# A two-layer hybrid decoder step: cached latents expanded by plain fp32 products, and four loops of small products in another order

## The chip, the core and the metric

The kernel runs on one core of a Trainium2 chip: TensorE (PE in the profile; PEld is its weight load), VectorE (DVE), ScalarE (ACT), GpSimd (POOL) and SyncE (SP), which here only issues transfers. The metric is the device time of one execution in microseconds, lower is better. The programs are compared by the median of several runs.

## What is computed

One inference step of two layers for 256 prompt tokens and 64 sample tokens (8 sequences of 8), model width 1024. Each layer projects its input for four mixers (latent attention, a convolution module, spatial gating and RWKV-7), projects their outputs back, and adds cross-attention to a memory and a gated feed-forward. Two pieces matter here. The sample tokens attend to 2048 cached positions each, which lie as latent rows of 512 columns in pages of 128 behind a page table; keys are expanded from the latents and normalised per head:

```python
def mla_expand(ckv, p):
    k_nope = rmsnorm((ckv @ p['mla_w_uk']).reshape(*lead, MLA_HEADS, QK_NOPE), p['mla_gk_nope'])
    v = (ckv @ p['mla_w_uv']).reshape(*lead, MLA_HEADS, V_DIM)

def mla_scores(q_nope, q_pe, k_nope, kpe):
    s = jnp.einsum('bqhd,bkhd->bhqk', q_nope, k_nope) + jnp.einsum('bqhr,bkr->bhqk', q_pe, kpe)
    return s.astype(jnp.float32) * MLA_SCALE

    def page_step(carry, phys):            # in mla_attend_sample, scanned over the page table
        m, l, acc = carry
        ckv_p = cache_ckv[phys, layer]
        kpe_p = cache_kpe[phys, layer]
        kn_p, v_p = mla_expand(ckv_p, p)
        sp = mla_scores(q_nope, q_pe, kn_p, kpe_p)
        m_new = jnp.maximum(m, jnp.max(sp, axis=-1, keepdims=True))
        corr = jnp.exp(m - m_new)
        ep = jnp.exp(sp - m_new)
        ...
```

And the sample tokens attend to 256 cached memory tokens with 4 heads of 128:

```python
    s = jnp.einsum('bthd,bmhd->bhtm', q, mem_k).astype(jnp.float32) * (X_HEAD_DIM ** -0.5)
    pr = jax.nn.softmax(s, axis=-1)
    xo = jnp.einsum('bhtm,bmhd->bthd', pr.astype(mem_v.dtype), mem_v)
```

All inputs and outputs are fp32.

## The kernel before

A layer goes through these stages: the combined projection and the mixers (rows by tag N, R, A, B, C), the scan of the paged cache with the rest of the mixers put between its steps (tags S and A), the output projection, cross-attention (tags X, Y and W; for the prompt's memory K and M) and the feed-forward (F). Dense products run in fp32r: a matrix is split into a high and a low part, and a product is the sum of three (high by high, low by high, high by low); `split` and `halves` make the parts with a ScalarE cast and a subtraction on VectorE or GpSimd. Products whose operands are plain fp32 tiles appear in the profile as two records each.

The scan (`mla_sample`, L1298) makes 8 steps in each layer, (g, Q) with g a half of the sequences and Q a quarter of their pages. `scan(g, Q)` takes 4 sequences j. For each it fetches the page rows (`Scb`, an indirect transfer issued by GpSimd, L1326) and the transposed latents (`Sckt`, 128x512, four transfers of 64 KB issued by SyncE, L1332, after the page numbers are read into registers). It casts the latents to fp32r (`Sckh`, ScalarE, L1336) and subtracts for the low part (`Sckl`, GpSimd, L397). For u in 0, 1 (two heads each) and j it expands them by three fp32r products into `pS`, and ScalarE squares the result into `Ssq`; the squares are summed per head by a product with 32 columns of weights into `pZ` (pZ<-Ssq), at partitions 32j to 32j + 31, so that the four j use four column groups of the array. The scores come from a second 32-column product, pZ<-Sckt. VectorE and ScalarE turn both into the scores `Sra`.

`attend` adds the rotary scores (16 products pA<-Scb,Akeep of 32 columns by 128), takes the running maximum and the exponentials, transposes them (pA<-fix,Sra), copies them to `Ak` (L1419) and multiplies them by the page rows (16 products pA<-Scb,Ak). `scan` of the next step is issued before `attend` of this one. The other mixers' VectorE work of that time is above all the causal convolution, one accumulation into `Bkeep` per tap (L401 for the prompt, L1000 for the samples).

In cross-attention the samples' queries are multiplied by cached memory keys (L1584: 16 products of 32 columns by 256 for each of two halves, pY and pZ<-u,Xm) and the weights by cached memory values (L1598: pY<-u,Ycc and pZ<-u,Wcc, 32 by 512). Both kinds of tile come through a ring of 13 buffers, `u`. The RWKV state loop (L877) makes 32 small products from the state of the sample sequences.

The order on each engine is set by a scheduler, from the program order and the waits that it models; `hold` keeps an instruction back in the schedule without a wait on the chip.

Of the kernel before, what the change touches and what calls it, by code (L numbers as in the profile page):

```python
# [10 lines left out]
F32 = mybir.dt.float32  # L11
# [12 lines left out]
NT = 320  # L24
# [297 lines left out]
def body(nc, tc, a, nl=L):  # L322
# [10 lines left out]
    BUFS = dict(u=13, wr=3, wh=4, wl=4, Nh=8, Nf=2, Nsm=2, Fh=8, Ff=4, Fsm=2, Xh=8, Xm=5, Xf=2, Xk2=2, Xcc=2, Xsm=8, Yk2=2, Ycc=2, Ysm=2,  # L333
# [24 lines left out]
    def block(tag, n):  # L358
        """one tile for what lives as long; returns what hands out its columns"""
# [20 lines left out]
    def in_order(first, last):  # L380
        """keeps the streamed products in program order among themselves"""
        after(first, dense_last[0])
        dense_last[0] = last
# [3 lines left out]
    def hold(ins, prev):  # L387
        """not before prev, by the schedule alone"""
        if prev is not None:
            tc.add_manual_dep(ins.ins, prev.ins.name, LATER, reason="held back")  # L390
# [43 lines left out]
    def keep(n):  # L434
        """columns held for the whole launch"""
# [29 lines left out]
    def rsq(e, now=False):  # L465
        """e <- e ** -0.5"""
# [12 lines left out]
    def split(hi, lo, src, scale=None, eng=None):  # L479
        """hi + lo = src * scale, both in fp32r"""  # L480
# [7 lines left out]
    def halves(raw, spans, scales=None, pool=()):  # L488
        """raw: a loaded tile, spans: column ranges -> (hi, lo) for each"""
# [15 lines left out]
    def wload(l, nm, idx, K):  # L505
        """one chunk of weights: a list of (hi, lo) [128, C] for its K row tiles"""
# [55 lines left out]
    def norm_pre(gain, wide=True):  # L562
        hs = []
        for k in range(8):
            h = sb("h", [128, 2, NT], F32R)
# [23 lines left out]
    def late():  # L589
        """what the first products do not need"""  # L590
# [7 lines left out]
    def group_norm_T(oj, vec, g, tag="F"):  # L598
        """oj: token rows [128, 256] x 3 -> split transposes of the normalised, scaled rows, [128, 2, NT] x 2"""
# [18 lines left out]
    def layernorm64(yj, eps):  # L618
        """per token and 64 columns, in place, without gain"""
# [48 lines left out]
    def rwkv(l, xs, vec):  # L668
# [45 lines left out]
        # normalised removal key  # L714
# [26 lines left out]
        # bonus  # L741
# [20 lines left out]
        # token rows of v, b and k  # L762
# [28 lines left out]
        # products between steps of a chunk  # L791
# [22 lines left out]
        # inverse of the unit triangular blocks by doubling  # L814
# [19 lines left out]
        for lev in (2, 4, 8, 16, 32):  # L834
# [4 lines left out]
            for q in qs:  # L839
# [5 lines left out]
                # the blocks of this level: rows of the first halves, columns of the second  # L845
# [19 lines left out]
        # state, chunk by chunk  # L865
# [7 lines left out]
        for c in (4, 0, 1, 2, 3):  # L873
            qs = None
            if c == 4:
                pq = [ps("T"), ps("T")]
                for hf in range(2):  # L877
                    R = Br[hf]
                    for i in range(2):
                        for b in range(8):  # L880
# [63 lines left out]
    def rwkv_out(l, vec, y, lng, lnb, vt, bon, tg, g2):  # L944
        # head norm, bonus, gate
# [13 lines left out]
    def sigmoid(t, scale=1.0, src=None):  # L959
        """t <- 1 / (1 + exp(scale * src))"""  # L960
# [141 lines left out]
    def mla(l, pj, vec):  # L1102
# [40 lines left out]
        # queries, keys and values  # L1143
# [67 lines left out]
        # sample queries against latents  # L1211
# [68 lines left out]
    class Side:  # L1280
        """work that is put between the steps of another"""
# [16 lines left out]
    def mla_sample(l, vec, t, side):  # L1298
        rq, qp, qz, ckT, kpT, ckn, ukv = (t[n] for n in ("rq", "qp", "qz", "ckT", "kpT", "ckn", "ukv"))
        oT = t["take"](4, 64)  # L1300
        u2 = sb("uk", [128, 2, 256], F32R)
        uh, ul = u2[:, 0], u2[:, 1]
        hold(S.copy(uh, ukv[:, 0:256]), pages[0])
        tt(ul, ukv[:, 0:256], uh.bitcast(F32), SUB)
# [4 lines left out]
        lows = []  # L1309

        def scan(g, Q):
            """page rows, and their scores without the rotary part"""
            ch[0] = "S"
            cbs, cks, ckhl = [], [], []
# [5 lines left out]
            for ld in loads:  # L1320
                hold(ld, lows[-BUFS["Sckt"]] if len(lows) >= BUFS["Sckt"] else cpage)
            for j in range(4):
# [12 lines left out]
                hi, lo = sb("ckh", [128, 512], F32R), sb("ckl", [128, 512], F32R)  # L1335
                S.copy(hi, ck)  # L1336
                lows.append(tt(lo, ck, hi.bitcast(F32), SUB, G if j in [0, 1, 2, 3] else V))
                ckhl.append((hi, lo))
            pn = ps("Z")
            for u in range(2):  # L1340
                sqs = []
                us = slice(128 * u, 128 * u + 128)
                for j in range(4):
                    p = ps("F")
                    hi, lo = ckhl[j]
                    mm(p, uh[:, us], hi, True, False)
                    mm(p, ul[:, us], hi, False, False)
                    mm(p, uh[:, us], lo, False, True)
# [53 lines left out]
        def attend(g, d, cbs, ra):  # L1402
            nb, ls, acc = d["nb"], d["ls"], d["acc"]
            p = ps("F")
            for j in range(4):
# [361 lines left out]
```

## Time and profile before

| | |
|---|---|
| runs, median of 3 | 1381.34 us (1374.33 to 1381.94) |
| span of the profiled execution | 1383.1 us |
| busy share PE, PEld, DVE, ACT, POOL | 96%, 81%, 70%, 47%, 16% |
| mean granted TensorE clock | 0.970 |
| mean traffic | 137 GB/s, 189.52 MB |

The profile shows one execution; its times are counted from the first instruction. "Busy" is the time in which at least one instruction of a kind ran; a matmul's end is modelled, so that records in steady flow overlap, and what one costs is read from start to start.

### The profile page before, as it was taken

What the parts mean: (1) busy time and instruction counts of PE and PEld (TensorE: products, weight loads), DVE (VectorE), ACT (ScalarE), POOL (GpSimd) and SP (SyncE); (2) the same over time, 40 slices, a digit from 0 to 9 for tenths busy, and PEclk for the clock granted to TensorE, in tenths of its full rate; (3) what the DMA queues carried; (4) which work ended last, traced back from release to release, by engine and by line L of the source; (5) the groups of instructions that cost most, each with busy time, mean ns of one, the idle gap of its engine ahead of it and who ended that gap; (6) DMA issues with size and microseconds to landing.
All of it is one profiled execution on the core that took longest, in us unless ns stands there. A gap on an engine that the chain in (4) does not pass through costs nothing.

```text
span 1383.1 us, 25248 instructions
## 1 busy us (share of the span) xinstructions
PE 1330.9 (96%) x9032; PEld 1113.5 (81%) x9032; DVE 962.2 (70%) x2414; ACT 651.6 (47%) x1425; POOL 217.5 (16%) x280
## 2 busy tenths in 40 slices
PE   5999999999999999999999899999999989999998
PEld 5859765566796799999998597755668959999998
DVE  6879468767786666566786894698777957655663
ACT  4443236667554544434444432375674635442441
POOL 1201313553000000000012113135540000000000
PEclk9999799999999999999999997999999999999999
DMA  7320313454475544444652204134563823444433
GB/s 233 125 77 15 118 44 89 140 159 145 146 253 191 177 157 145 154 153 151 201 171 94 81 11 123 42 88 133 162 215 143 296 93 137 147 144 153 153 115 107
DMA packets 105486, 189.52 MB, mean 137 GB/s; under 512 B 21393, under 2 KB 58642, under 8 KB 105362
## 3 DMA queue, kind: packets, MB, share of 16 engines
q1 hardware_dynamic: 91040, 157.84, 34.6%
q0 software_dynamic: 5120, 20.98, 5.0%
q10 hardware_dynamic: 9202, 9.11, 2.3%
q8 instruction: 71, 1.16, 0.3%
q14 instruction: 53, 0.43, 0.1%
HBM read 182.12 MB, written 5.75 MB: 136 GB/s over the span
## 4 chain that ended last, share of the span: by engine, by line
PE 52%; issue 9%; DVE 2%; POOL 1%; DMA 1%; ACT 0%; SPq 0%; POOLq 0%; ACTq 0%
PE pD L375 38%; PE pR L375 5%; PE pS L375 2%; PE pA L375 2%; PE pZ L375 2%; PE pA L460 1%; DMA Sckt<-in_ckvT 1%; PE pR L460 0%; DVE Bkeep L401 0%; DVE u L401 0%; PE pE L460 0%; POOL Sckl L397 0%; DVE Ccv L401 0%; DVE u L397 0%; DVE Sz L401 0%
## 5 line engine op out<-in xcount | busy, mean ns | idle before, releaser
L482 ACT CAST wh<-wr 128x512 fp32r<-128x512 f32 (+1 forms) x448 | 252.4, 601 | 133.0 <-PE pD L375 83.9
L375 PE MATMUL pD<-Fh,wh 128*128 128x320 f32 x1408 | 310.5, 309 | 0.0
L397 DVE TENSOR_TENSOR wl<-wr,wh 128x512 fp32r<-128x512 f32 (+1 forms) x448 | 291.7, 674 | 11.4 <-ACT wh L482 9.8
L375 PEld LDWEIGHTS pD<-Fh,wh 128*128 128x128 f32 x1408 | 235.7, 188 | 0.0
L375 PE MATMUL pD<-Fh,wl 128*128 128x320 f32 x704 | 217.5, 309 | 0.0
L375 PE MATMUL pD<-u,wh 128*128 128x320 f32 x704 | 154.9, 309 | 0.0
L375 PEld LDWEIGHTS pD<-Fh,wl 128*128 128x128 f32 x704 | 132.2, 188 | 0.0
L375 PEld LDWEIGHTS pD<-u,wh 128*128 128x128 f32 x704 | 117.8, 188 | 0.0
L397 DVE TENSOR_TENSOR Ff<-pD,fix 128x320 f32<-128x320 f32 x88 | 43.2, 491 | 103.3 <-PE pD L375 100.9
L375 PE MATMUL pD<-u,wl 128*128 128x320 f32 x352 | 108.8, 309 | 0.0
L375 PE MATMUL pD<-Nh,wh 128*128 128x320 f32 x384 | 94.6, 326 | 13.8 <-ACT wh L482 13.8
L413 ACT ACTIVATE u<-Ff 128x320 fp32r<-128x320 f32 x44 | 20.8, 472 | 176.1 <-DVE Ff L397 176.1
L397 POOL TENSOR_TENSOR Sckl<-Sckt,Sckh 128x512 fp32r<-128x512 f32 x64 | 85.8, 1351 | 108.7 <-ACT Sckh L1336 91.7
L375 PE MATMUL pS<-Sckh,Auk 128*128 128x512 f32 x256 | 92.0, 432 | 4.3 <-DVE Sra L401 1.8
L413 ACT ACTIVATE Ssq<-pS 128x512 f32<-128x512 f32 x128 | 73.5, 594 | 45.3 <-PE pS L375 38.6
L397 DVE TENSOR_TENSOR fix<-fix,pD 128x320 f32<-128x320 f32 x80 | 38.8, 485 | 73.0 <-PE pD L375 72.3
L375 PEld LDWEIGHTS pD<-Nh,wh 128*128 128x128 f32 x384 | 66.8, 194 | 19.6 <-ACT wh L482 13.8
L375 PEld LDWEIGHTS pS<-Sckh,Auk 128*128 128x128 f32 x256 | 47.3, 197 | 36.4 <-issue 22.1
L401 DVE SCALAR_TENSOR_TENSOR Bkeep<-Bkeep,fix 128x256 f32<-128x256 f32 x120 | 74.5, 624 | 0.6
L1326 POOL DMA_INDIRECT Scb<-in_ckv,fix x64 | 63.4, 991 | 63.4 <-PE pR L375 23.3
L375 PE MATMUL pZ<-Ssq,fix 128*32 128x512 f32 x256 | 71.9, 654 | 1.3 <-ACT Sra L414 0.9
L375 PEld LDWEIGHTS pD<-u,wl 128*128 128x128 f32 x352 | 66.1, 188 | 0.0
(478 smaller groups left out, 2580.7 us busy)
## 6 DMA issues: line engine op xcount, KB each, us to landing
wr<-in_w SPq DMA_DIRECT2D x200, 512.0 KB
Sckt<-in_ckvT SPq DMA_DIRECT2D x256, 64.0 KB
u<-in_memK SPq DMA_DIRECT2D x32, 256.0 KB
u<-in_memV SPq DMA_DIRECT2D x32, 256.0 KB
wr<-in_w SPq DMA_DIRECT2D x16, 384.0 KB
wr<-in_memT SPq DMA_DIRECT2D x12, 256.0 KB
wr<-in_w SPq DMA_DIRECT2D x8, 352.0 KB
Rmk<-in_cst ACTq DMA_DIRECT2D x2, 704.0 KB
```

The costliest lines, as they stand in the source:

```text
L375: return T.matmul(out, lhsT=lhsT, rhs=rhs, start=start, stop=stop)
L397: return (eng or V).tensor_tensor(out=out, in0=in0, in1=in1, op=op)
L401: return V.scalar_tensor_tensor(out=out, in0=in0, scalar=scalar, in1=in1, op0=op0, op1=op1)
L413: return S.activation(out, in_, func, bias=bias, scale=scale)
L460: T.transpose(out, in_, ident[:n, :n])
L482: S.copy(hi, src)
L1326: ld = nc.gpsimd.indirect_dma_start(out=cb.rearrange("p i c -> p (i c)"), out_offset=None, in_=a["ckv"], in_offset=off)
```

## The change

1. The latents are expanded by one plain fp32 product with the weights as they are (`ukv`), instead of three fp32r products. The casts `Sckh`, the subtractions `Sckl` and the split of the weights (`Auk`) are gone: 64 casts on ScalarE, 64 subtractions on GpSimd and, once in each layer, a cast and a subtraction for the weights.
2. The loops of the rotary scores, of the memory keys, of the memory values and of the RWKV state products have their inner and outer loops exchanged, so that products which follow each other write to different 32-column (or 64-column) parts of the array. For the keys, four tiles are now loaded ahead of the eight products that read them.
3. The register loads of page numbers are held behind the score of two steps back instead of the low part of twelve tiles back.
4. The eight tiles of a normalised input are one tile with eight parts.

```diff
+        hall = sb("h", [128, 8, 2, NT], F32R)
         for k in range(8):
-            h = sb("h", [128, 2, NT], F32R)
+            h = hall[:, k]
...
-                for hf in range(2):
-                    R = Br[hf]
-                    for i in range(2):
-                        for b in range(8):
+                for i in range(2):
+                    for b in range(8):
+                        for hf in range(2):
+                            R = Br[hf]
...
-        u2 = sb("uk", [128, 2, 256], F32R)
-        uh, ul = u2[:, 0], u2[:, 1]
-        hold(S.copy(uh, ukv[:, 0:256]), pages[0])
-        tt(ul, ukv[:, 0:256], uh.bitcast(F32), SUB)
...
             for ld in loads:
-                hold(ld, lows[-BUFS["Sckt"]] if len(lows) >= BUFS["Sckt"] else cpage)
+                hold(ld, scored[-2] if len(scored) - base >= 2 else cpage)
...
-                hi, lo = sb("ckh", [128, 512], F32R), sb("ckl", [128, 512], F32R)
-                S.copy(hi, ck)
-                lows.append(tt(lo, ck, hi.bitcast(F32), SUB, G if j in [0, 1, 2, 3] else V))
-                ckhl.append((hi, lo))
...
-                    hi, lo = ckhl[j]
-                    mm(p, uh[:, us], hi, True, False)
-                    mm(p, ul[:, us], hi, False, False)
-                    mm(p, uh[:, us], lo, False, True)
+                    mm(p, ukv[:, us], cks[j])
...
-            for j in range(4):
-                for n in range(4):
+
+            for n in range(4):
+                for j in range(4):
                     mm(p[32 * j : 32 * j + 32, n * 128 : n * 128 + 128], qz[:, 4 * g + j, n], cbs[j][:, 4])
...
-                for j in range(4):
-                    for h2 in range(2):
+
+                for h2 in range(2):
+                    kbs = []
+                    for j in range(4):
                         kb = sb("u", [128, 512])
                         hold(nc.sync.dma_start(kb, a["memK"][l, 4 * g + j, :, h2 * 512 : h2 * 512 + 512]), ahead)
-                        for hh in range(2):
-                            h = 2 * h2 + hh
-                            mm(p[32 * j : 32 * j + 32, 0:256], qpad[g][:, j, h], kb[:, hh * 256 : hh * 256 + 256], h == 0, h == 3)
+                        kbs.append(kb)
+                    for hh in range(2):
+                        h = 2 * h2 + hh
+                        for j in range(4):
+                            mm(p[32 * j : 32 * j + 32, 0:256], qpad[g][:, j, h], kbs[j][:, hh * 256 : hh * 256 + 256], h == 0, h == 3)
...
-                for j in range(4):
-                    for m in range(2):
+                for m in range(2):
+                    for j in range(4):
                         vb = sb("u", [128, 512])
```

What the scheduler makes of it is read from the order of instructions; three places follow. The first is TensorE in layer 0, from the expansion for the third scan step (pS) to the rotary scores of the first attend (pA<-Scb,Akeep; Scb_2035 to Scb_2068 are the rows of the four sequences, x4 is four products in a row). Before:

```order
L375 MATMUL pS<-Sckh_2504,Auk_1999 128x512 x2
L375 MATMUL pS<-Sckl_2505,Auk_1999 128x512
L375 MATMUL pS<-Sckh_2471,Auk_1999 128x512 x2
L460 MATMUL pA<-fix,As_2202 64x128
L375 MATMUL pS<-Sckl_2472,Auk_1999 128x512
L375 MATMUL pS<-Sckh_2482,Auk_1999 128x512 x2
L375 MATMUL pZ<-Ssq_2513,fix 32x512
L375 MATMUL pA<-Akeep_1313,As_2206 128x128
L375 MATMUL pA<-Scb_2035,Akeep_1313 32x128 x4
L375 MATMUL pA<-Scb_2046,Akeep_1313 32x128 x4
L375 MATMUL pA<-Scb_2057,Akeep_1313 32x128 x4
L375 MATMUL pA<-Scb_2068,Akeep_1313 32x128 x4
```

After:

```order
L375 MATMUL pS<-Sckt_2392,Akeep_1306 128x512
L375 MATMUL pZ<-Ssq_2421,fix 32x512
L375 MATMUL pS<-Sckt_2399,Akeep_1306 128x512
L460 MATMUL pA<-fix,As_2160 64x128
L375 MATMUL pZ<-Sckt_2392,Akeep_1306 32x512
L375 MATMUL pA<-Akeep_1306,As_2164 128x128
L375 MATMUL pA<-Scb_2025,Akeep_1306 32x128
L375 MATMUL pA<-Scb_2032,Akeep_1306 32x128
L375 MATMUL pA<-Scb_2039,Akeep_1306 32x128
L375 MATMUL pA<-Scb_2046,Akeep_1306 32x128
L375 MATMUL pA<-Scb_2025,Akeep_1306 32x128
L375 MATMUL pA<-Scb_2032,Akeep_1306 32x128
```

The rotary products now go round the four sequences; the expansion is one product, and single 32-column products (pZ) stand between the full ones. The second place is TensorE in layer 0 at the memory keys (u_5005 and so on are key tiles, Xm the padded queries). Before:

```order
L375 MATMUL pY<-u_5009,Xm_4652 32x256
L375 MATMUL pY<-u_5013,Xm_4652 32x256 x2
L375 MATMUL pY<-u_5017,Xm_4652 32x256 x2
L375 MATMUL pY<-u_5021,Xm_4652 32x256 x2
L375 MATMUL pY<-u_5025,Xm_4652 32x256 x2
```

After:

```order
L375 MATMUL pY<-u_4724,Xm_4379 32x256
L375 MATMUL pY<-u_4726,Xm_4379 32x256
L375 MATMUL pY<-u_4728,Xm_4379 32x256
L375 MATMUL pY<-u_4730,Xm_4379 32x256
L375 MATMUL pY<-u_4724,Xm_4379 32x256
L375 MATMUL pY<-u_4726,Xm_4379 32x256
L375 MATMUL pY<-u_4728,Xm_4379 32x256
L375 MATMUL pY<-u_4730,Xm_4379 32x256
```

Two neighbours used to read one tile and write one column group; now four neighbours read four tiles. The third place is GpSimd in layer 0 from the low parts for the fifth scan step on (Sckl) to the page rows of later steps (Scb). Before:

```order
L397 TENSOR_TENSOR Sckl_2937<-Sckt_2931,Sckh_2936 128x512
L1326 DMA Scb_2464<-in_ckv,fix 128x640
L1326 DMA Scb_2475<-in_ckv,fix 128x640
L1326 DMA Scb_2486<-in_ckv,fix 128x640
L1326 DMA Scb_2497<-in_ckv,fix 128x640
L397 TENSOR_TENSOR Csm_2850<-Csm_2850,fix 128x3
L397 TENSOR_TENSOR Sckl_2948<-Sckt_2942,Sckh_2947 128x512
```

After:

```order
L397 TENSOR_TENSOR Rsm_1910<-Rsm_1910,fix 128x12
L397 TENSOR_TENSOR Csm_2712<-Csm_2712,fix 128x3
L1323 DMA Scb_2390<-in_ckv,fix 128x640
L1323 DMA Scb_2397<-in_ckv,fix 128x640
L1323 DMA Scb_2404<-in_ckv,fix 128x640
```

Between the indirect transfers only small operations are left on GpSimd.

## Rows read from the trace of the kernel before

**Rows 1.** Section 1 of the page: busy us (share of the span) xinstructions.

```profile
PE 1330.9 (96%) x9032; PEld 1113.5 (81%) x9032; DVE 962.2 (70%) x2414; ACT 651.6 (47%) x1425; POOL 217.5 (16%) x280
```

**Rows 2.** By stage: stretch, length, busy us of PE, PEld, DVE, ACT, POOL, clock, DMA share, GB/s.

```profile
280.00:320.00 40.00, 36.54 (x287) 22.80 (x282) 24.61 (x50) 23.36 (x49) 22.58 (x21) 0.91 0.63 177
...
920.00:960.00 40.00, 36.76 (x282) 22.35 (x284) 36.43 (x75) 23.89 (x55) 22.38 (x18) 0.94 0.33 95
```

**Rows 3.** PE's waits, 183 to 352 us: us in total, times, longest.

```profile
PE pS L375 <- DVE Sra L401: 1.0, 1, 1.0
PE pA L460 <- ACT Sra L414: 0.9, 1, 0.9
...
PE pE L460 <- DVE Bg L397: 0.7, 1, 0.7
PE pS L375 <- ACT Sckh L1336: 0.6, 1, 0.6
```

**Rows 4.** PE's waits, 883 to 1058 us.

```profile
PE pA L375 <- DVE Ak L1419: 3.2, 1, 3.2
...
PE pS L375 <- DVE Sra L401: 0.8, 1, 0.8
```

**Rows 5.** Order of time, VectorE, then GpSimd: start us, us, instruction, xcount [idle before].

```profile
947.59 3.36 DVE L401 SCALAR_TENSOR_TENSOR Bkeep<-Bkeep,fix 128x256 f32<-128x256 f32 x1
...
948.13 2.53 POOL L397 TENSOR_TENSOR Sckl<-Sckt,Sckh 128x512 fp32r<-128x512 f32 x2
```

**Rows 6.** Tile Bkeep (ns min/median/max); then the page's group (busy us, mean ns).

```profile
L401 DVE SCALAR_TENSOR_TENSOR Bkeep<-Bkeep,fix x120: 443/475/3360, 175.7 to 985.1; 128x256 f32<-128x256 f32 x120
...
L401 DVE SCALAR_TENSOR_TENSOR Bkeep<-Bkeep,fix 128x256 f32<-128x256 f32 x120 | 74.5, 624 | 0.6
```

**Rows 7.** Order of time, PE, at an expansion: two triples of fp32r products begin.

```profile
282.50 0.62 PE L375 MATMUL pS<-Sckh,Auk 128*128 128x512 f32 x2
...
283.19 0.62 PE L375 MATMUL pS<-Sckh,Auk 128*128 128x512 f32 x2
```

**Rows 8.** Order of time, PE, at a plain fp32 product of that shape.

```profile
83.34 1.02 PE L375 MATMUL pA<-Akeep 128*128 128x512 f32 x2
...
84.43 0.40 PE L375 MATMUL pD<-wl,Nh 128*64 128x512 f32 x1
```

**Rows 9.** Order of time, PE, at memory values and at products with page rows.

```profile
1040.38 1.08 PE L375 MATMUL pA<-Scb,Ak 128*32 128x128 f32 x32
1041.39 0.73 PE L375 MATMUL pK<-wh,Mh 128*128 128x512 f32 x2
...
1119.29 1.94 PE L375 MATMUL pY<-u,Ycc 128*32 128x512 f32 x16
1121.06 1.06 PE L375 MATMUL pZ<-u,Xm 128*32 128x256 f32 x8
```

**Rows 10.** Page, groups of instructions: busy us, mean ns, idle before and its releaser.

```profile
L397 POOL TENSOR_TENSOR Sckl<-Sckt,Sckh 128x512 fp32r<-128x512 f32 x64 | 85.8, 1351 | 108.7 <-ACT Sckh L1336 91.7
...
L413 ACT ACTIVATE Ssq<-pS 128x512 f32<-128x512 f32 x128 | 73.5, 594 | 45.3 <-PE pS L375 38.6
```

**Rows 11.** Groups of PE's instructions by line and shape, columns as in rows 10.

```profile
L375 PE MATMUL pA<-Scb,Akeep 128*32 128x128 f32 x512 | 42.8, 278 | 0.2
L375 PE MATMUL pA<-Scb,Ak 128*32 128x128 f32 x512 | 20.3, 297 | 4.0 <-DVE Ak L1419 4.0
L375 PE MATMUL pY<-u,Xm 128*32 128x256 f32 x64 | 12.4, 384 | 0.0
L375 PE MATMUL pZ<-u,Xm 128*32 128x256 f32 x64 | 12.1, 382 | 0.1
...
L375 PE MATMUL pY<-u,Ycc 128*32 128x512 f32 x32 | 3.9, 598 | 0.0
```

**Rows 12.** By stage in layer 1's cross-attention, columns as in rows 2.

```profile
1100.00:1110.00 10.00, 10.00 (x71) 6.47 (x70) 6.17 (x29) 2.93 (x10) 0.00 (x0) 1.00 1.00 364
...
1120.00:1131.00 11.00, 8.44 (x59) 3.81 (x51) 3.62 (x13) 4.03 (x11) 0.00 (x0) 1.00 0.00 0
```

More of the change, by code (lines that the diff above doesn't have):

```diff
@@ L332, in body @@
     RINGS = ("u", "Scb", "Sckt", "Sckh", "Sckl", "Ssq", "Sra", "Sz", "Ff", "Fh", "Nf", "Mf")
-    BUFS = dict(u=13, wr=3, wh=4, wl=4, Nh=8, Nf=2, Nsm=2, Fh=8, Ff=4, Fsm=2, Xh=8, Xm=5, Xf=2, Xk2=2, Xcc=2, Xsm=8, Yk2=2, Ycc=2, Ysm=2,
+    BUFS = dict(u=13, wr=3, wh=4, wl=4, Nh=1, Nf=2, Nsm=2, Fh=1, Ff=4, Fsm=2, Xh=1, Xm=5, Xf=2, Xk2=2, Xcc=2, Xsm=8, Yk2=2, Ycc=2, Ysm=2,
                 Rkeep=1, Rh=6, Rf=3, Rg1=3, Rk2=3, Rcc=3, Rs2=2, Rst=2, Rsh=1, Rsm=4,
@@ L1300, in mla_sample @@
         oT = t["take"](4, 64)
-        u2 = sb("uk", [128, 2, 256], F32R)
-        uh, ul = u2[:, 0], u2[:, 1]
-        hold(S.copy(uh, ukv[:, 0:256]), pages[0])
-        tt(ul, ukv[:, 0:256], uh.bitcast(F32), SUB)
         qf = lambda b: qp[:, b].rearrange("p h t -> p (h t)")
         PG = [0, 0, 3, 3]
-        lows = []
+        base = len(scored)
         def scan(g, Q):
             ch[0] = "S"
-            cbs, cks, ckhl = [], [], []
+            cbs, cks = [], []
             cpage = pages[[0, 2, 3, 3][min(2 * Q + g, 3)]]
```

## The prediction

> **What bounds the kernel now.** I read the page first. TensorE (PE) is busy for 96% of 1383.1 us and VectorE, ScalarE and GpSimd for 70, 47 and 16% [rows 1], so a change counts by what it takes from PE or adds to it, and by the waits of PE that it moves. Next I read the table by stage, for the stretches in which the kernel goes through the paged cache ("the scan" below; 183 to 352 us and 883 to 1058 us are the windows read). There PE is not full: 36.54 us of 280 to 320 and 36.76 of 920 to 960, and the granted clock is 0.91 and 0.94 there [rows 2]. A clock c over T us costs about T x (1 - c), since for part of T it is granted the lower level, 1.2 of 2.4 GHz, and work goes at half speed: 3.6 and 2.4 us for the two rows. Third, the waits of PE in the scan, by what ended them [rows 3, 4]: three rows of layer 0 name VectorE (1.0 to 0.7, together 2.5 us) and five of layer 1 (3.2 to 0.8, together 6.8 us), so 9.3 us in all. Rows that name ScalarE, six and four, come to another 6.3 us, from 0.9 down; one of 0.6 names the cast that the change removes.
>
> Why is VectorE late, when it is no more than 70% busy? The order of time shows it: an accumulation into Bkeep that has a median of 475 ns takes 3.36 us at 947.59, while GpSimd makes two of the Sckl tiles from 948.13 on [rows 5]. The longest of the 120 is this 3360 ns, and their mean is 624 ns, so this line alone is 120 x 0.149 = 17.9 us above its median [rows 6]. Adding up, over the trace, what VectorE's instructions take above the median of their own kind, I find 40 us in 44 instructions, and all 44 lie over an Sckl subtraction. The Ak copy that PE waits for (3.2 us) stands in VectorE's queue behind such a stretch.
>
> **The change part by part.** *Expansion of the latents.* Three fp32r products give way to one plain fp32 product, 128 times. In steady flow a triple starts every 283.19 - 282.50 = 0.69 us [rows 7], 0.23 us a product. A plain fp32 product of the same shape (128x512, weights 128x128, two records) stands elsewhere in the kernel: from its start at 83.34 to 84.43 lie it and one fp32r product, 1.09 us, so it takes 1.09 - 0.23 = 0.86 us [rows 8]. That is 0.17 us dearer: 128 x 0.17 = **+21.8 us**. Bounds: the pair is listed with 1.02 us from its first start to its last end, so if nothing overlapped its end the term would be 128 x 0.33 = +42; below 0.86 it can't go as long as PE has other work to take, since that row is steady flow already, and where PE stands still beside it the waits below take the difference up. I take 21.8.
>
> *Norm and score products (pZ, 32 columns of the array).* Their count is the same, but they are placed otherwise. Four that follow each other use four column groups and run as one pass: eight in pY<-u,Ycc take 1121.06 - 1119.29 = 1.77 us, 0.89 a pass [rows 9]. I counted passes over both program orders, a pass being a run without another kind of product between and without a column group twice: 35 before and 45 after in layer 0, 35 and 49 in layer 1. 24 x 0.89 = **+21.4 us**; the bound below is half, where PE would have sat waiting for the squares anyway. The array changes between 32-column and full products 71 times in each layer before, 79 and 91 after. One change back costs about 0.12 us: the 32 small records from 1040.38 fill 1.01 us [rows 9], and eight steps of a quarter of 0.44 us (half of 0.89) make 0.89. So 28 x 0.12 = **+3.4 us**. The Trainium skill, TensorEngine Tiling (Array Packing), section Key Properties, says that a change of tiling mode drains the engine; this speaks against the new order, and the trace agrees in sign, with 0.12 us a change. Also, six more norm products stand right behind the product that feeds their square. A square takes 594 ns [rows 10], so 0 to 3.6 us; I take **+2 us**.
>
> *Casts and subtractions.* 64 Sckh casts on ScalarE and 64 Sckl subtractions on GpSimd (85.8 us) go [rows 10]. They overlap PE, so their own time counts nothing; what comes back is what waited behind them. Of VectorE's 9.3 us I give back **-8 us** (one wait of 0.8 is for the RWKV mixer); of ScalarE's 6.3, whose queue gets shorter, **-3 us**; and the clock of the stretches 280 to 320 and 920 to 960, which falls right behind such waits, 3.6 + 2.4 = **-6 us** [rows 2]. Bounds: nothing of it, or all, 9.3 + 6.3 + 6.0 = 21.6 us. What is late next is then the chain of softmax, ScalarE's exponentials before the transposes, not the subtraction.
>
> *Rotary scores (pA<-Scb,Akeep).* 16 loops, whose order now cycles through the four column groups. The products with the values (pA<-Scb,Ak) have the same shape and count and already cycle: 20.3 us busy against 42.8 [rows 11]. **-22.5 us**; in the new order 15 of the 16 loops stand unbroken, so little of it is in doubt.
>
> *Cached memory keys (pY and pZ<-u,Xm).* 128 records of 256 columns, 12.4 + 12.1 = 24.5 us [rows 11]. The memory values run four at once: 32 records of 512 columns in 3.9 us, so 64 of 256 also 3.9, and 128 of them 7.8. Gain at most 16.7; the new order breaks some blocks, so that I count 24 passes for the 16 that are needed, eight more of 0.44 us, which leaves 13.2. In layer 1 the transfers are full until 1110 (share 1.00), and there PE may get ahead of its tiles; none is left after 1120 [rows 12]. I take off 1 more: **-12 us**, bounds -6 (half) and -13.2.
>
> *No term.* The values' loop already runs four at once (above), and in the RWKV state loop the program order is what it was: the scheduler had and has one half behind the other. The page-number loads now come after the score two scans back; that leaves one scan, some 20 us (a window of 170 holds eight), for its 16 loads of 64 KB, 1 MB, which the transfers move in about 3 us at 364 GB/s [rows 12].
>
> Sum: 21.8 + 21.4 + 3.4 + 2 - 8 - 3 - 6 - 22.5 - 12 = -2.9 us. The profiled span of 1383.1 is 1.8 above the runs' median of 1381.34; the difference is taken off the median: **1378 us** after rounding.
>
> **The rivals.** A measurement here can tell about 1% (13.8 us) from no change. (a) *Faster*: the new passes fall into time in which PE waited for squares anyway (10.7 instead of 21.4) and all the waits and clock come back: 21.8 + 10.7 + 3.4 - 21.6 - 22.5 - 13.2 = -21, **1360 us**. For it: all 44 long VectorE instructions have one cause, and it goes. The Trainium skill, SBUF — State Buffer, section SBUF: two separate sides, calls the port pair of VectorE and GpSimd an exclusive lock held for the whole instruction, for VectorE instructions with two SBUF inputs; the trace agrees, 3.36 us against 0.475. Against it: the waits named for VectorE are 9.3 us, not 40. (b) *Slower*: in the scan the norm pass is the new wait. Each single norm product takes a pass for itself and waits for its square, and PE is the limit there, so that no wait comes back: 21.8 + 21.4 + 3.4 + 3.6 - 22.5 - 6 = +22, **1403 us**. For it: +50 us of dearer work is certain, and its relief rests on waits; against it: the waits shown are caused by what is removed. It decides once less than 8 of the 17 us of waits and clock come back while the memory keys give 6. (c) *The turned loops don't do what they say*: the keys wait for transfers and the rotary loops gain half: the sum is then -2.9 + 11 + 6 = +14, 1395, the edge of "slower".
>
> **How the numbers follow.** The forecast, within 1% (1367 to 1395), 0.50; (a) and what lies toward it 0.31; (b) and (c) 0.19. The likeliest case alone is 1368 to 1391. The range goes a little past (a), which holds its clearest part, and to the edge of (c): 1356 to 1396; what lies beyond it is most of (b) and a tail of (a), some 0.18.
>
> **What would show it.** Right: pS<- Sckt at 0.86 us a product; the Bkeep line with a maximum near its median; pA<-Scb,Akeep near 20 us and pY and pZ<-u,Xm near 11 together; the clock 1.00 in the stretches that follow the waits. Wrong: pS records with gaps, waits of PE for Ssq by the dozen, PE waiting for loads of Sckt or of memory keys, or a Bkeep line still at 600 ns.

## The result, and the profile after

| | before | after |
|---|---|---|
| median of 20 runs each | 1379.89 us | 1387.07 us (1381.79 to 1396.14) |
| ratio to before, 95% interval | 1 | 1.0062 (1.0043 to 1.0081) |
| span of the profiled execution | 1383.1 us | 1384.6 us |
| mean granted clock | 0.970 | 0.979 |

The changed kernel is 0.6% slower, 8.6 us by the ratio: within 1% and inside the range, but on the other side of no change from the -2.9 us of the sum. Here is TensorE's work after, first section 1 of the page (as [rows 1]), then three stretches (columns as in [rows 2]):

```profile
PE 1337.6 (97%) x8904; PEld 1061.7 (77%) x8904; DVE 921.6 (67%) x2412; ACT 627.2 (45%) x1359; POOL 131.1 (9%) x216
```

```profile
280.00:320.00 40.00, 39.56 (x261) 16.24 (x261) 12.82 (x29) 20.78 (x40) 11.12 (x12) 1.00 0.59 175
...
920.00:960.00 40.00, 37.25 (x273) 15.77 (x271) 31.57 (x85) 18.75 (x39) 6.79 (x7) 1.00 0.51 154
...
1110.00:1120.00 10.00, 8.94 (x42) 3.62 (x44) 2.94 (x14) 1.34 (x5) 0.00 (x0) 0.66 0.56 191
```

In the two stretches of the scan the clock is 1.00 (it was 0.91 and 0.94) and PE is fuller by 3.0 and 0.5 us. The third, at the memory keys of layer 1, has a new dip to 0.66. VectorE's accumulation into Bkeep, the tile and its group (as [rows 6]):

```profile
L401 DVE SCALAR_TENSOR_TENSOR Bkeep<-Bkeep,fix x120: 448/478/485, 179.4 to 963.8; 128x256 f32<-128x256 f32 x120
```

```profile
L401 DVE SCALAR_TENSOR_TENSOR Bkeep<-Bkeep,fix 128x256 f32<-128x256 f32 x120 | 56.7, 476 | 0.0
```

The longest of the 120 is 485 ns instead of 3360. PE's waits, 183 to 365 us and then 880 to 1058 us (as [rows 3, 4]):

```profile
PE pZ L375 <- DVE Asm L401: 1.0, 1, 1.0
...
PE pZ L375 <- ACT Ssq L413: 1.0, 1, 1.0
...
PE pA L375 <- DVE Akeep L397: 0.8, 1, 0.8
PE pZ L375 <- DVE Bkeep L401: 0.7, 1, 0.7
```

```profile
PE pZ L375 <- ACT Ssq L413: 2.3, 2, 1.5
PE pA L375 <- DVE Akeep L1424: 1.1, 1, 1.1
```

VectorE is named with 3.6 us (2.5 and 1.1) instead of 9.3, and the Ak copy is no longer among them. So most of what was to be relieved was relieved, and the kernel is slower. Groups of PE's instructions (as [rows 10, 11]):

```profile
L375 PE MATMUL pS<-Sckt,Akeep 128*128 128x512 f32 x256 | 130.9, 621 | 1.8 <-DMA Sckt<-in_ckvT 0.9 <-PE pZ L375 0.8
L375 PE MATMUL pZ<-Ssq,fix 128*32 128x512 f32 x256 | 80.6, 603 | 5.0 <-ACT Ssq L413 3.2 <-DVE Asm L401 1.0 <-DVE Bkeep L401 0.7
L375 PE MATMUL pA<-Scb,Akeep 128*32 128x128 f32 x512 | 27.2, 276 | 0.0
L375 PE MATMUL pA<-Scb,Ak 128*32 128x128 f32 x512 | 18.0, 276 | 0.1
L375 PE MATMUL pZ<-u,Xm 128*32 128x256 f32 x64 | 9.0, 437 | 0.6 <-issue 0.6
L375 PE MATMUL pY<-u,Xm 128*32 128x256 f32 x64 | 5.5, 386 | 0.0
```

The rotary scores went from 42.8 to 27.2, not to 20.3, the keys from 24.5 to 14.5. Since busy times of neighbours overlap, I use from here on "own time": for each record of PE the time from its start to the start of the next one, added up by kind, over the scans of both layers. It also holds the time in which PE stood still behind a record, and what a lower clock added.

| own time, us | pS | pZ<-Ssq | pZ<-Sckt | rotary |
|---|---|---|---|---|
| before | 115.5 | 60.6 | 22.5 | 41.4 |
| after | 128.4 | 62.3 | 27.1 | 25.4 |
| e3 (one-tile norm input) | 110.2 | 59.8 | 19.4 | 42.6 |
| e1 (e3 and turned loops) | 109.5 | 65.4 | 19.8 | 24.8 |
| e2 (e3 and plain fp32) | 125.9 | 62.3 | 26.3 | 39.8 |
| e9 (e3, grouped) | 112.8 | 55.3 | 20.0 | 41.6 |
| e11 (e2, grouped) | 122.4 | 36.8 | 21.2 | 39.1 |
| e7 (after, grouped) | 124.3 | 37.4 | 20.3 | 24.3 |

### The profile page after: what moved, and what is told of

The parts are those of the page before. It is cut to its first block, busy times and chain, and to the rows that moved or that the text cites. A ratio compares the mean times of both kernels' runs of the same rounds, so it can differ in the third digit from the quotient of the medians.

```text
span 1384.6 us, 24573 instructions
## 1 busy us (share of the span) xinstructions
PE 1337.6 (97%) x8904; PEld 1061.7 (77%) x8904; DVE 921.6 (67%) x2412; ACT 627.2 (45%) x1359; POOL 131.1 (9%) x216
## 4 chain that ended last, share of the span: by engine, by line
PE 82%; issue 8%; DVE 3%; DMA 3%; ACT 1%; POOL 1%; SPq 1%; POOLq 0%; DVEq 0%; ACTq 0%
PE pD L375 48%; PE pR L375 10%; PE pS L375 7%; PE pZ L375 6%; PE pA L375 4%; PE pK L375 2%; PE pA L460 1%; DMA u<-in_memV 1%; DMA wr<-in_memT 1%; PE pR L460 1%; PE pX L375 1%; DVE u L401 1%; PE pE L460 1%; PE pE L375 1%; DMA Bkeep<-in_convh 0%
## 5 line engine op out<-in xcount | busy, mean ns | idle before, releaser
L482 ACT CAST wh<-wr 128x512 fp32r<-128x512 f32 (+1 forms) x448 | 257.6, 603 | 272.4 <-PE pD L375 188.9
L375 PE MATMUL pS<-Sckt,Akeep 128*128 128x512 f32 x256 | 130.9, 621 | 1.8 <-DMA Sckt<-in_ckvT 0.9
L375 PE MATMUL pZ<-Ssq,fix 128*32 128x512 f32 x256 | 80.6, 603 | 5.0 <-ACT Ssq L413 3.2
L375 PEld LDWEIGHTS pS<-Sckt,Akeep 128*128 128x128 f32 x256 | 42.8, 192 | 55.2 <-issue 37.6
L375 PE MATMUL pD<-Nh,wl 128*128 128x320 f32 x192 | 62.9, 327 | 2.2 <-DVE wl L397 2.2
L375 PE MATMUL pD<-wh,Nh 128*128 128x352 f32 (+3 forms) x192 | 59.2, 382 | 0.2 <-ACT u L413 0.2
```

The lines of the kernel that those rows point to most:

```text
L375: return T.matmul(out, lhsT=lhsT, rhs=rhs, start=start, stop=stop)
L482: S.copy(hi, src)
```

## The experiments

Each was timed in five rounds beside the kernel before on its own chip, and ratios are to that; 0.1% is 1.4 us, and "x% below e3" is a difference of two such ratios. Letters in the quoted expectations stand for theories; what each comes to is said in words behind it. The kernels come in four sets of four that shared a chip: e1 to e4, e5 to e8, e9 to e12, e13 to e16. The kernel before took 1379.8, 1384.0, 1388.2 and 1384.7 us on the four chips.

### The parts alone (e1 to e4)

e3 is the kernel before with the one-tile input of the norm and nothing else (its ring holds one such tile instead of eight small ones, as many columns):

```diff
+        hall = sb("h", [128, 8, 2, NT], F32R)
-            h = sb("h", [128, 2, NT], F32R)
+            h = hall[:, k]
```

> Only the one-tile norm input is changed, everything else as before. Theory A and B: nothing, ratio 1.000 within 0.002. Rival C (the single tile adds waits at the start of each normalised projection; in the changed kernel's trace layer 0 is 3.3 us later at its first expansion): +3 to +5 us, ratio 1.002 to 1.004.

Measured 0.996 (0.9938 to 0.9981). The part that should cost nothing gave 0.4%, 5.5 us, and not the loss of rival C; e1, e2 and e4 have it too, so they are compared with e3. By the traces PE's records stand in another order in places, most of them in the last part of each scan. The clock goes with it: its mean over all runs is 0.9763 in e3 and 0.9736 in the kernel before beside it, which by T x (1 - c) is 32.6 and 36.4 us, 3.8 of the 5.5. Why the order and the clock changed I did not settle.

e1 adds the four turned loops, of which this is the rotary one:

```diff
-            for j in range(4):
-                for n in range(4):
+            for n in range(4):
+                for j in range(4):
                     mm(p[32 * j : 32 * j + 32, n * 128 : n * 128 + 128], qz[:, 4 * g + j, n], cbs[j][:, 4])
```

> The four turned loops and the one-tile norm input, with the three fp32r products, casts and subtractions of before. Theory A (the loops gain what PE saves in them, and the plain expansion then costs more than its relief returns): by the trace of the changed kernel the rotary loops take 25.4 us instead of 41.4 and the keys 16.3 instead of 24.7, so about 24 us under before, ratio 0.982. Theory B (the expansion is about even and it is the loops that lose their gain, in waits for softmax and for key tiles): within 5 us of before, ratio 0.997 to 1.003.

Measured 0.9837 (0.9806 to 0.9869), as theory A said against the kernel before; against e3 it is 1.2% less, 17 us.

e4 is e3 with this loop alone turned.

> Only the rotary loop turned (and the one-tile norm input), fp32r expansion as before. Theory A: -16 us, as the 16 loops take 25.4 us instead of 41.4, ratio 0.988. Theory B: -5 to 0 us, because PE then waits for the exponentials that it used to cover.

Measured 0.9877 (0.9849 to 0.9905), again theory A's ratio; 0.8% below e3, 11.5 us, where its own time fell by 17.3. On the same chip e1 lies 0.4% under e4, 5.5 us (the intervals overlap), which is what the other three loops gave together.

e2 is e3 with the plain fp32 expansion, all loops as before. The later load of page numbers comes with it, since the low parts that the old hold names are gone; PE waits for latents (Sckt) for 0.9 us in all in the changed kernel, by the group of pS above.

```diff
-                    mm(p, uh[:, us], hi, True, False)
-                    mm(p, ul[:, us], hi, False, False)
-                    mm(p, uh[:, us], lo, False, True)
+                    mm(p, ukv[:, us], cks[j])
```

> The plain fp32 expansion without any turned loop (with the one-tile norm input and the later load of page numbers). Theory A: it carries the loss and the loops hide it, +7 + 24 = about 31 us over before, ratio 1.022; VectorE's long instructions are gone all the same. Theory B: about +5 us, ratio 1.004.

Measured 1.0165 (1.0136 to 1.0193), 2.05% above e3: 28 us, between the two theories and nearer A. With the loops turned (the changed kernel against e1) it is 2.25%, 31 us. The parts add up: -5.5 (e3), -17 (e1 against e3), +31 (after against e1) make the +8.5 of the whole.

### What the casts and subtractions were worth (e5, e8)

e5 is e2 with the 64 casts and 64 GpSimd subtractions made all the same, their results unused:

```diff
+                hi, lo = sb("ckh", [128, 512], F32R), sb("ckl", [128, 512], F32R)
+                S.copy(hi, ck)
+                tt(lo, ck, hi.bitcast(F32), SUB, G)
```

> The plain fp32 expansion without turned loops, and beside it the 64 casts and 64 GpSimd subtractions of before, whose results nothing reads. Theory A (the dearer products cost about 41 us in all, and 14 come back because the casts and subtractions are gone): the 14 are lost again, 1402 + 14 = 1416 us, ratio 1.026. Rival D (what comes back is small, the dearer products cost about 27 in all): 1402 to 1405 us, ratio 1.016 to 1.018.

Measured 1.0194 (1.0153 to 1.0235), 0.3% above e2, some 4 us with intervals that overlap: nearer rival D than A. VectorE's long instructions are back in it: what its instructions take above the median of their kind is some 26 us in over 30 instructions (40 us in the kernel before, none in the changed kernel). Since nothing reads the results, e5 prices the load on the two engines and their collision, not the chain from the latents over cast and subtraction to the product.

e8 is e1 with the subtractions on VectorE instead of GpSimd, so that the two engines can't meet there:

```diff
-                lows.append(tt(lo, ck, hi.bitcast(F32), SUB, G if j in [0, 1, 2, 3] else V))
+                lows.append(tt(lo, ck, hi.bitcast(F32), SUB, V))
```

> Four turned loops with the fp32r expansion, the low parts made by VectorE instead of GpSimd. Theory A: VectorE's 36 us of overlong instructions go, but 64 subtractions of about 0.68 us, 43 us, come: as the loops alone, 1358 us within 4, ratio 0.984. Rival H (what hurts is the single long stall in front of a wait of TensorE, and short ones more in number do not): 1345 us, ratio 0.975.

Measured 0.9815 (0.9774 to 0.9856), theory A's 0.984 and not to be told from e1's 0.9837. The tile Bkeep in e1 and then in e8 (min/median/max):

```profile
L401 DVE SCALAR_TENSOR_TENSOR Bkeep<-Bkeep,fix x120: 449/475/2054, 175.5 to 962.2; 128x256 f32<-128x256 f32 x120
```

```profile
L401 DVE SCALAR_TENSOR_TENSOR Bkeep<-Bkeep,fix x120: 463/476/483, 180.1 to 991.4; 128x256 f32<-128x256 f32 x120
```

The stalls vanish (2054 to 483 ns) and the time doesn't move. But VectorE takes on the 64 subtractions, and PE now waits for it in another place, 191 to 351 us in e8:

```profile
PE pZ L375 <- DVE Sra L401: 4.1, 2, 3.6
```

So e8 is a net, behind which a gain can hide. That the stalls cost a few us at most rests on e5; e8 does not contradict it.

### How the small products stand in the order (e7, e9 to e11)

The schedule of e7 keeps the four norm products of each u behind the last square of that u, and the score products behind the norm products; nothing else differs from the changed kernel:

```diff
-                    act(sq, p, AF.Square)
+                    held = act(sq, p, AF.Square)
...
-                    mm(pn[32 * j : 32 * j + 32], C("hsum")[:, 32 * u : 32 * u + 32], sqs[j], u == 0, u == 1)
+                    last = mm(pn[32 * j : 32 * j + 32], C("hsum")[:, 32 * u : 32 * u + 32], sqs[j], u == 0, u == 1)
+                    hold(last, held)
...
-                mm(p[32 * j : 32 * j + 32], qf(4 * g + j), cks[j])
+                hold(mm(p[32 * j : 32 * j + 32], qf(4 * g + j), cks[j]), last)
```

> The changed kernel, with the norm products held by the schedule until all four squares are made, and the score products behind the norms: 30 and 29 passes of 32-column products instead of 44 and 48, and 112 changes of array mode instead of 170. Theory A (each pass takes 0.89 us of TensorE, but grouping makes it wait for squares part of that time): about half of 33 x 0.89, -15, so 1372 us, ratio 0.994. Rival G (single passes lie in time in which TensorE waits anyway): no change, 1387 us, ratio 1.005. If every pass counts fully: 1355 us, ratio 0.982.

Measured 0.9789 (0.9749 to 0.9829): 2.7% below the changed kernel, 38 us. That is more than any theory gave; the interval takes in the 0.982 of every pass counted fully, and neither A nor G. By the table of own times pZ<-Ssq loses 24.9 us, pZ<-Sckt 6.8 and pS 4.1, together 35.8: nearly all of it. In the same stretch of time, order of time on PE, first the changed kernel, then e7:

```profile
283.98 2.84 PE L375 MATMUL pS<-Sckt,Akeep 128*128 128x512 f32 x6
286.76 1.37 PE L375 MATMUL pZ<-Ssq,fix 128*32 128x512 f32 x7
287.64 0.39 PE L375 MATMUL pA<-Scb,Akeep 128*32 128x128 f32 x6
287.97 0.59 PE L375 MATMUL pZ<-Ssq,fix 128*32 128x512 f32 x1
288.40 0.59 PE L375 MATMUL pZ<-Sckt,Akeep 128*32 128x512 f32 x1
```

```profile
286.69 1.03 PE L375 MATMUL pZ<-Ssq,fix 128*32 128x512 f32 x6
287.65 2.84 PE L375 MATMUL pS<-Sckt,Akeep 128*128 128x512 f32 x6
```

Six records of pS (three products) take 286.76 - 283.98 = 2.78 us. Behind them the changed kernel's small products come in runs of seven, six and one record, and a lone record takes 0.43 us (288.40 - 287.97); in e7 six of them take 0.96 together.

e11 is e2, e9 is e3 and e10 is e1 with the same lines.

> Plain fp32 expansion, loops not turned, grouped: 30 and 29 passes instead of 44 and 48, 112 changes instead of 170. Theory P: 33 x 0.89 + 58 x 0.12 = -36 against the plain expansion alone, ratio 0.990; the difference to the grouped fp32r kernel is then what the expansion itself costs without its fragments, about 0 to +18 us. Rival Q: as P here, but with the grouped fp32r kernel 30 us lower than this one.

> fp32r expansion, loops not turned, one-tile norm input, with the norm and score products grouped by the schedule: 31 and 32 passes of 32-column products instead of 34 and 37, and 114 changes of array mode instead of 144. Theory P (a pass costs 0.89 us and a change of mode 0.12 wherever they stand): 8 x 0.89 + 30 x 0.12 = -11 against the one-tile kernel, ratio 0.988. Rival Q (grouping is worth as much as in the changed kernel, for another reason, such as the wait for a single square): -30, ratio 0.975.

> The same grouping with the four loops turned, fp32r expansion: 30 and 32 passes instead of 34 and 37, 118 changes instead of 140. Theory P: 9 x 0.89 + 22 x 0.12 = -11 against the loops alone, 1347 us, ratio 0.976. Rival Q: -30, 1328 us, ratio 0.962.

| ratio to before | as it was | grouped |
|---|---|---|
| fp32r, loops not turned | 0.996 (e3) | 0.9991 (0.9968 to 1.0014) (e9) |
| fp32r, loops turned | 0.9837 (e1) | 0.9877 (0.9843 to 0.9910) (e10) |
| plain fp32, not turned | 1.0165 (e2) | 0.9873 (0.9847 to 0.9900) (e11) |
| plain fp32, turned | 1.0062 (after) | 0.9789 (e7) |

Grouping is worth 2.7 to 2.9% with plain fp32 and nothing with fp32r (0.3 and 0.4% to the bad, across sets). e9 and e10 meet neither P nor Q. e11 has P's ratio within its interval, but lies under e9, where P had it level or above. With fp32r there are fewer passes to save, 71 to 63 for both layers against 92 to 59 with plain fp32 (the counts quoted above, by one rule; the prediction counted 94 for the changed kernel), and the hold takes 4.5 us off pZ<-Ssq (59.8 to 55.3) instead of 25 (62.3 to 36.8).

That is not all of it. For the two scans of each profile, from the first expansion to the last product with page rows, here is the time that PE stood still, and what the clock cost it while it worked, by T x (1 - c):

| idle / clock, us | as it was | grouped |
|---|---|---|
| fp32r, loops not turned | 13.1 / 6.6 (e3) | 24.1 / 17.8 (e9) |
| fp32r, loops turned | 15.2 / 6.7 (e1) | 27.2 / 23.0 (e10) |
| plain fp32, not turned | 6.9 / 3.4 (e2) | 11.0 / 4.0 (e11) |
| plain fp32, turned | 9.7 / 1.7 (after) | 12.1 / 4.2 (e7) |

Without idle time and at the full clock, the two pZ kinds fall by 12 and 14 us with fp32r and by 30 and 33 with plain fp32. So grouping saves PE's work with fp32r too, and waits and a lower clock take it back; why PE waits more there the runs don't show. The clocks of all runs agree: beside the kernel before, the clock cost 6 and 10 us more in e9 and e10, 15 and 4 us less in e11 and e7.

So plain fp32 costs 2.05 to 2.25% as it was scheduled, and gains 1.2% (e11 against e9, 16 us) and 0.9% (e7 against e10, 12 us) when its small products stay together. That gain does not show cheaper products: the clock alone differs by 21 and 14 us between these pairs.

### Where the turned loops' gain went (e6, e13 to e16)

e6 is e3 with the memory keys alone turned; e15 has that in layer 0 only, e16 in layer 1 only:

```diff
-                for j in range(4):
-                    for h2 in range(2):
+                for h2 in range(2):
+                    kbs = []
+                    for j in range(4):
...
+                    for hh in range(2):
+                        h = 2 * h2 + hh
+                        for j in range(4):
```

> Only the memory keys' loop turned (and the one-tile norm input), fp32r expansion. Theory A: 6 us gained in layer 0, where the memory's projection gives TensorE other work, and 1 lost in layer 1, where it then waits for VectorE's Qk and its clock falls: 1374.5 - 5 = 1370 us, ratio 0.993. Rival F (the keys gain 12 as forecast, and the rotary loops are what falls short when both are turned): 1363 us, ratio 0.988.

> The one-tile kernel with the memory keys' loop turned in layer 0 only. Theory A: 6 us under the one-tile kernel, as in layer 0 the memory's projection fills TensorE, ratio 0.992. Rival U (the time saved there is given back later in the layer): 0.996.

> The same with the loop turned in layer 1 only. Theory A: 0 to 5 us above the one-tile kernel, ratio 0.996 to 0.9995, with TensorE waiting for VectorE's Qk and a granted clock below 1.00 behind it. Rival F (4 to 6 us gained in each layer): 0.992.

Measured 0.9957 (0.9935 to 0.9978), 0.9956 (0.9932 to 0.9980) and 0.9991 (0.9966 to 1.0016), against e3's 0.996: no gain to be seen in the first two, and perhaps a loss of 4 us in the third. e6 meets neither theory, e15 has rival U's number, e16 lies in theory A's range. These ratios come from three chips and each difference is known to some 4 us, so that the 5.5 us of e1 against e4 on one chip is not contradicted. The keys' own time does fall, in the changed kernel from 11.8 to 5.6 us in layer 0 and from 12.9 to 10.7 in layer 1. In layer 1 PE runs ahead of the other side of the attention, order of time on PE in the changed kernel:

```profile
1108.01 0.40 PE L375 MATMUL pX<-fix,Xm 128*64 128x1 f32 x8
1109.05 0.63 PE L375 MATMUL pZ<-u,Xm 128*32 128x256 f32 x4 [0.64 <-issue]
1111.06 0.69 PE L460 MATMUL pX<-fix,Qk 128*128 128x128 f32 x2 [1.38 <-DVE Qk L407]
```

PE stands 0.64 and 1.38 us within three, and there the ten us with the clock at 0.66 begin, which by T x (1 - c) cost 3.4 us. Turning the keys brings this wait in e6 too; here the row for it of 1060 to 1140 us in e3, then in e6:

```profile
PE pX L460 <- DVE Qk L407: 0.9, 1, 0.9
```

```profile
PE pX L460 <- DVE Qk L407: 2.9, 2, 1.5
```

In e6 the keys of layer 1 have 3.0 us less own time than in e3 (9.8 instead of 12.8) and 2.0 us more of this wait. From the first product on Xh to the first on Xo layer 1 takes 46.0 us in e6 and 46.7 in e16, against 48.4 in e3 and 47.1 in the kernel before: a gain of 0.4 to 2.4 us there, so that this wait takes most of it, and what e16 lost lies elsewhere. (e6 has the waits, 0.63 and 1.38 us, without the dip: its clock is 1.00 there.) In layer 0 the same stretch is shorter by 5 to 6 us (58.2 in e3, 53.4 in e6, 52.3 in e15), yet the whole is not. The two scans of these profiles take 9 to 12 us more than the 326.1 in e3 (335.5 in e6, 335.6 in e15, 338.5 in e16), with PE idle in them for 17.7, 18.4 and 20.9 us instead of 13.1. Part of this may be the chip, as the kernel before took 4 to 5 us more on theirs than on e3's; I found no cause in the change. This stays open.

e13 leaves the rotary products and the addition of their result out. e14 is e4 with the rotary loop made twice:

```diff
             for n in range(4):
                 for j in range(4):
                     mm(p[32 * j : 32 * j + 32, n * 128 : n * 128 + 128], qz[:, 4 * g + j, n], cbs[j][:, 4])
+            for n in range(4):
+                for j in range(4):
+                    mm(p[32 * j : 32 * j + 32, n * 128 : n * 128 + 128], qz[:, 4 * g + j, n], cbs[j][:, 4])
```

> The one-tile kernel (fp32r expansion, loops not turned) with the 16 rotary loops and the additions of their result left out, so that the scores lack their rotary part. The loops take 42.6 us of TensorE's time in that kernel's profile; the order has also 8 passes less, 7 us. Theory S (TensorE's time there is worth its full length): -50 against the one-tile kernel, ratio 0.960. Theory T (a microsecond saved there returns about two thirds, the rest goes into waits for VectorE and ScalarE, which set the pace of the softmax): about -33, ratio 0.972.

> The rotary loop turned and made twice (the second writes the same values again), fp32r expansion. The second loop follows the first directly and so runs in step: 16 x 0.9 = 14 us more of TensorE. Theory S: 1362 + 14 = 1376 on the scale of the first runs, ratio 0.998. Theory T: two thirds of it, +9, ratio 0.994; if time there were free, 0.988.

e13: 0.9751 (0.9712 to 0.9791), 2.1% below e3, near theory T and away from S. So 42.6 us of own time taken away, with 16 additions on VectorE, give 29 back, a share of 0.68, as e4's 11.5 of 17.3 are 0.66. Where the rest goes is seen in the own times: without the rotary products pS rises from 110.2 to 119.2 and pZ<-Sckt from 19.4 to 27.8, +17.4 together (pZ<-Ssq falls by 3.0). The rise of pS is time that PE stands still behind it (4.4 us in e3, 13.3 in e13), above all for VectorE's copy Ak; here its row in layer 0's scan in e3, 188 to 353 us, then in e13, 189 to 335 us:

```profile
PE pA L375 <- DVE Ak L1421: 1.0, 1, 1.0
```

```profile
PE pA L375 <- DVE Ak L1415: 4.4, 3, 1.9
```

The rise of pZ<-Sckt holds no such time, and its cause is not shown. In e4 it is pZ<-Ssq that rises, 59.8 to 65.2, of which 3.8 us is time that PE stands still.

e14: 1.0096 (1.0059 to 1.0133), 2.2% above e4, 30 us, more than any theory gave, and the own time of the loops went from 25.3 to 52.8. By the rate of an unbroken loop, 0.9 to 1.0 us, the second set of 16 loops should have cost some 15 us; it cost 27.5. The group's line and the order of time on PE in e14:

```profile
L375 PE MATMUL pA<-Scb,Akeep 128*32 128x128 f32 x1024 | 46.1, 275 | 8.0 <-issue 8.0
```

```profile
262.20 1.58 PE L375 MATMUL pA<-Scb,Akeep 128*32 128x128 f32 x47
264.02 0.30 PE L375 MATMUL pA<-Scb,Akeep 128*32 128x128 f32 x2 [0.24 <-issue]
264.74 0.28 PE L375 MATMUL pA<-Scb,Akeep 128*32 128x128 f32 x1 [0.41 <-issue]
265.45 0.45 PE L375 MATMUL pA<-Scb,Akeep 128*32 128x128 f32 x4 [0.43 <-issue]
266.19 0.39 PE L375 MATMUL pA<-Scb,Akeep 128*32 128x128 f32 x2 [0.29 <-issue]
...
268.41 0.42 PE L375 MATMUL pA<-Scb,Akeep 128*32 128x128 f32 x1 [0.45 <-issue]
```

47 records fill 1.6 us, then PE stands 0.24 to 0.45 us before every one to four records and waits for nothing that the profile shows.

### A version that is faster than both (e12)

e12 is e7 with the keys turned in layer 0 alone (the key loop under `if l == 0:`, in layer 1 as before).

> The grouped changed kernel with the memory keys' loop turned in layer 0 only. Theory A (in layer 1 the turned keys hand their time to waits for Qk and a slower clock): 0 to 3 us under the grouped kernel, ratio 0.977 to 0.979. Rival F (the turned keys gain 4 to 6 us in each layer): 4 to 6 us above it, ratio 0.982.

Measured 0.9754 (0.9723 to 0.9784), 34 us below the kernel before and within theory A's reach, not F's. Its interval overlaps that of e7, so the step from e7 is not shown.

## Why the prediction was wrong, point by point

**The turned loops: the step that failed.** The sum had -22.5 for the rotary scores and -12 for the keys, -34.5. Measured: -11.5 for the rotary loop alone, nothing to be seen for the keys alone, and -12 to -17 for all four (e1 against e3 -17, after against e2 -14, e10 against e9 -16, e7 against e11 -12). That is about 20 us short and by itself turns -2.9 into a loss. It failed in two places.

First, the own time. The prediction took the busy time of the values' loops as what a turned loop takes and said that "15 of the 16 loops stand unbroken, so little of it is in doubt". The count was of products between; what stands ahead of a loop was left out. The changed kernel, order of time on PE:

```profile
250.67 0.61 PE L375 MATMUL pZ<-Ssq,fix 128*32 128x512 f32 x3
250.75 0.27 PE L375 MATMUL pA<-Scb,Ak 128*32 128x128 f32 x1
250.86 0.38 PE L375 MATMUL pA<-Scb,Akeep 128*32 128x128 f32 x2
251.10 0.60 PE L375 MATMUL pZ<-Ssq,fix 128*32 128x512 f32 x3
251.53 0.60 PE L375 MATMUL pZ<-Sckt,Akeep 128*32 128x512 f32 x3
251.55 0.41 PE L375 MATMUL pA<-Scb,Akeep 128*32 128x128 f32 x2
251.96 0.60 PE L375 MATMUL pZ<-Sckt,Akeep 128*32 128x512 f32 x3
252.39 1.05 PE L375 MATMUL pA<-Scb,Akeep 128*32 128x128 f32 x28
...
282.12 1.08 PE L375 MATMUL pA<-Scb,Ak 128*32 128x128 f32 x32
283.03 1.02 PE L375 MATMUL pZ<-Ssq,fix 128*32 128x512 f32 x2
```

A loop of 32 records behind a full product takes 0.91 us (282.12 to 283.03). A rotary loop starts beside single norm and score products of 512 columns, which go to one column group each; its first four records lie among them from 250.86 to 252.39, and only the last 28 go at the full rate, so it took 2.51 us until 253.37. The loops' own time became 25.4 instead of about 19.

Second, what an own time is worth. Half to two thirds of what PE saved in the turned loops reached the end; the sum had set it one for one, because PE "is busy for 96%". e13 shows it without any question of loops: 42.6 us taken away, 29 back. The rate is not the same everywhere: added work went one for one (e14: 27.5 us of own time, 30 us), and so did what e7 saved (35.8 us, 38).

**The expansion: the net was right by luck, the parts were not.** The sum had +31.6 net, measured +28 and +31. But the gross was over 48 (21.8 + 21.4 + 3.4 + 2), and the own times give +25: pS +15.7, pZ<-Ssq +2.5, pZ<-Sckt +6.9 (e2 against e3; +30 without idle time and at the full clock). In steady flow a plain product takes somewhat more than was said (2.78 / 3 = 0.93 us here, 0.86 by [rows 8]), but on average the fp32r triples did not run at their 0.69 us: with what stands between they took 110.2 / 128 = 0.86, the plain ones 0.98. Of the 21.4 us counted for new passes the own times of pZ have 9.4 (13 without idle time and at the full clock). Of rival (b), that a single norm product takes a pass for itself and waits for its square, e7 and e11 show the first half, with 38 and 40 us to be had by grouping; the waits for Ssq are 3.3 us in the changed kernel. The Trainium skill, TensorEngine Tiling (Array Packing), section Key Properties, says that a change of tiling mode drains the engine. With plain fp32 the runs agree in sign: the kernels with 112 such changes in the two scans (e7, e11) are faster than those with 170 (after, e2). With fp32r they don't show it (e9, 114 instead of 144, no gain), and no run parts that price from the passes'.

**The relief: -17 was too much.** The cause was read rightly. With the subtractions gone the longest Bkeep accumulation is 485 ns, the Ak wait of 3.2 us is gone, and the clock of the two stretches is 1.00. The price was not. From e3 to e2 PE's idle time in the scans falls by 6.2 us and the cost of the clock by 3.2, some 9 of the 17. Part had gone before: e3 still has the subtractions, and against the kernel before (17.7 / 14.8, as in the table of idle / clock) its profile has 4.6 and 8.2 us less, with 1.0 us of Ak waits left, so these waits and dips were not the subtractions' alone. Putting casts and subtractions back, with nothing that waits for them, cost some 4 us (e5). I had added waits of PE and clock as if nothing else were late in their place; in the changed kernel the waits for Ssq and Asm are, 4.3 us. This error and that of the gross price cancelled.

**No term.** The one-tile norm input was put at nothing and gave -5.5 us (e3). Rival (c) had the rotary loops gain half, which they did (11.5 of 22.5), and the keys wait, which they did in layer 1 (2.9 us for Qk). Its number was 1395; the measured time lies between it and the forecast, and the 5.5 us that had no term are part of that.

## What to carry to other kernels

Where small products use a part of the array, count in the scheduler's order how long their runs are, and what stands ahead of them: a lone record took 0.43 us where six in a run took 0.96, and holding them together was worth 38 us with plain fp32, more than the turned loops gave. With fp32r the same hold gave nothing, as waits and the clock took it back, so time it in the kernel at hand. A busy share of 96% does not mean that a us saved on that engine is a us off the end: remove the work altogether once, in a kernel that is only timed, and read the exchange rate (here two thirds) before adding up savings. Look at idle time and the granted clock beside the work saved, since both can take it back. When two large terms are to cancel, test each alone.

## What the runs showed of the hardware

Small products that run four at once can go faster than they are supplied: in e14, after 47 records in 1.6 us, the next came one to four at a time with 0.24 to 0.45 us before each, labelled "issue", so that 16 more loops cost 27.5 us instead of some 15. What supplies them too slowly the trace doesn't name. A lone 32-column product's record of 512 columns kept PE for 0.43 us where a run of six took 0.96 (e7 against the changed kernel).

The granted clock fell to 0.66 over ten us (1110 to 1120) in the changed kernel, after PE had stood for 0.64 and 1.38 us within three; the stretches of [rows 12] have 1.00. But e6 has the same two waits with a clock of 1.00 behind them, so the waits alone do not settle it.
